# A hybrid decoder layer on one core: mixer output and memory keys computed with one load of the high weights for both halves of the input

## The chip, the cores and the metric

The kernel runs on one core of one Trainium2 chip, in one launch. The metric is device microseconds of an execution; the number for a kernel is the median of its runs. Before the change it is 1819.08 us, the median of 3 runs from 1818.16 to 1819.49.

## The reference, cut to what matters

A layer for 256 tokens of width 2048, all in float32: a token mixer, cross-attention into 256 memory tokens, and a gated channel mixer, each between two root-mean-square norms and added to the residual stream `x`.

```python
h = rms_norm(x, mix_pre_norm)
merged = ...                                  # mLSTM and RWKV-7 branches, gated
y = merged @ w_mix_out                        # 2048 x 2048: the mixer output
x = x + rms_norm(y, mix_post_norm)
h = rms_norm(x, xattn_pre_norm)
m = rms_norm(mem, mem_norm)
k, v = split(m @ xattn_wkv)                   # 2048 x 512 each: the memory's keys and values
q = h @ xattn_wq
o = softmax(q k / sqrt(128)) v                # 4 heads of 128
x = x + rms_norm(o @ xattn_wo, xattn_post_norm)
h = rms_norm(x, ffn_pre_norm)
x = x + rms_norm((gelu(conv(h @ w_up_gate)) * conv(h @ w_up_up)) @ w_down, ffn_post_norm)
```

## The kernel before

Every large product is made of three. A float32 weight and a float32 input are each split into a high part and a low part of the type fp32r, and the kernel adds high weight x high input, high weight x low input, and low weight x high input. `Feed` (L373) brings the weights in pieces of 128 x 1024 numbers, called sources here: a DMA into `raw` (three buffers), then ACT casts `raw` to `wh` (L402, the high part), then DVE subtracts `wh` from `raw` into `wl` (L423, the low part); `wh` and `wl` have four buffers each, in tiles of 1024 + 128 columns (`staged`, L391). All matmuls go through the helper `mm`, so they stand at L189 in the profile.

The program is a list of blocks, run one after the other by `run` (L435). A block of kind `fm` makes 512 output features for all 256 tokens, features on the partitions, into two PSUM banks of the pool `acc`, which has four; for each of the 16 slices `k` of the input and each of 4 groups of 128 features it issues three matmuls of 256 columns, each with its own weight load (below, a narrow triple). A block of kind `tm` puts tokens on the partitions and moves weights, 512 columns at a time. A block with `wide` makes 256 features: for each slice and group it issues one matmul of 512 columns, high weights against high and low input side by side, and one of 256 columns, low weights against high input (a wide pair). A bank then holds high and low products apart, and they have to be added when they leave PSUM. Before the change only 58 blocks of the channel mixer's first product are wide (`w_fw`); their `fw_evac` (L1627) lets ACT copy the low half to SBUF (tile `ul`) and DVE add the high half from PSUM (tile `us`).

The stages that the text speaks of stand in this order, with the tiles that name them in the profile: the mixer output `w_mo` (four `fm` blocks over `mgh` and `mgl`, evacuated by `y_evac`, L1268, which also adds up squares for the norm, `sty`); the memory's keys `w_xk` (one `fm` block over `mx`, evacuated by `kx_evac` into `kT`); the queries `w_xq` (one `fm` block over `qh` and `ql`); the memory's values `w_xv` (one `tm` block over `mx`, evacuated into `xv`); the attention output `w_xo` (four `fm` blocks over `oT`); then the channel mixer.

Everything beside the matmuls is written as Python generators, whose pieces `run` lets out between matmuls. A call of `side.half` (L107) is a half step: there are two for each source, in narrow and in wide blocks. At a half step one piece of the first waiting evacuation is issued, if a budget of estimated DVE and ACT time allows it, and then one piece of each chain that is due. Each engine executes its instructions in the order in which they were issued.

Between the keys and the queries stands `Residual` (L1294). It waits until the sum of squares of the mixer output is done: `column_of_sums` (L344) adds the two halves of `sty` on DVE (`fold`), waits `n` half steps (1 unless told otherwise), issues the small matmuls `st`, a DVE and a GpSimd instruction, and waits one half step more; then `Residual` issues the matmuls `stb`. From there it issues a piece every two half steps. Each of its pieces 0 to 7 lets DVE scale two slices of the mixer output (`z`), add them to the residual stream (`xr`), and split the sum into two slices of the queries' input, `qh` on ACT and `ql` on DVE. While it runs, the same DVE also makes the `wl` of every source. When it is near its end, squares of the new residual stream are summed (`stx`), and after the queries the softmax of the four heads runs as a chain of pieces under the values' matmuls: scores `xsc`, exponentials `spr`, transposes `xpT`, a copy `pT` on ACT. `need_o` (L1559) makes the attention output wait for the softmax, for `xv`, and for the matmuls `xo`, whose result is split into `oT`.

Of the kernel before, what the change touches and what calls it, by code (L numbers as in the profile page):

```python
# [9 lines left out]
F32 = mybir.dt.float32  # L10
F32R = mybir.dt.float32r
# [141 lines left out]
def _layer(ctx, tc, nc, d, dbg):  # L153
# [15 lines left out]
    def big(name, shape=None, dt=F32):  # L169
        return mp.tile(shape or [P, KD, S], dt, tag="big", bufs=2, name=name)  # L170
# [97 lines left out]
    def times(out, ps, row):  # L268
# [2 lines left out]
            row = bc(row, ps.shape[1])  # L271
        dve.tensor_mul(apart(out), halves(ps), apart(row))

    def bc(ap, n):
        return ap.unsqueeze(1).broadcast_to((ap.shape[0], n, ap.shape[1]))

# [96 lines left out]
    class Feed:  # L373
# [16 lines left out]

        def staged(self, name, r):  # L391

            w = wp.tile([P, 1024 + 128], F32R, tag=name, bufs=4, name=name)
            k, c = r.shape[1:]
            return w[:, 0:k * c].rearrange("p (k c) -> p k c", k=k)

# [843 lines left out]
    def br_evac(i, cb):  # L1240
        def gen(ps):
            sg = M["sg", i, cb]
            if cb == 0 and i == 0:
                M["pa"] = [U("pa0", [P, D]), U("pa1", [P, D])]
            if cb == 0 and i == 1:
                M["mg"] = [big("mgh", dt=F32R), big("mgl", dt=F32R)]
            for t in range(2):
                pa = M["pa"][t][:, cb * 512:cb * 512 + 512]
                if i == 0:
                    dve.tensor_mul(pa, ps[t], sg[t])  # L1250
                else:
                    dve.tensor_mul(sg[t], ps[t], sg[t])
                    dve.tensor_add(sg[t], sg[t], pa)
                yield
            if i == 0:
                return
            yield
            for t in range(2):
                q = aux("mT", [P, 4, P])
                for j in range(4):  # L1260
                    pe.transpose(q[:, j], sg[t][:, j * P:(j + 1) * P], ident)
                mg = [apart(M["mg"][j][:, cb * 4:cb * 4 + 4])[:, :, :, t * 64:t * 64 + 64] for j in range(2)]
                split(mg[0], mg[1], halves(q))
                yield
        return gen


    def y_evac(b, st, key, gname):  # L1268

        def gen(ps):  # L1270
            if b == 0:
                M[key] = [U("z0"), U("z1")]
            z = M[key][b // 2]
            late = b == 3 and key == "z2"
            if late:
                st.add(ps[0])
                st.last(ps[1], "bg0")
                st.column()
            for g in range(2):
                if not late:  # L1280
                    st.add(ps[g])
                for j in range(2):
                    m = (b % 2) * 4 + g * 2 + j
                    act.activation(z[:, m], ps[g][:, j], AF.Copy, scale=pcol(gname, b * 4 + g * 2 + j))
                if g or not late:
                    yield
            if b == 3 and not late:
                yield from st.column_of_sums()
        return gen

    def part(v, k2):
# [118 lines left out]
    sty = Stat("sty")  # L1410
    stm = Stat("stm", "ysb0")

    def mem_prep():
        mx = hT("mx")
        M["mh"], M["ml"] = mx[:, 0], mx[:, 1]
        ts = []
        for c in range(10):
            if c % 2 == 0 and c < 8:
                ts.append(C("mem", f"bg{c // 2 % 2}", [P, 4, S]))
                sp.dma_start(ts[c // 2], d["mem"][:, c * 2:c * 2 + 4])  # L1420
            if c >= 2:
                t = ts[c // 2 - 1][:, c % 2 * 2:c % 2 * 2 + 2]
                for j in range(2):
                    k = c * 2 - 4 + j
                    split_gain(M["mh"][:, k], M["ml"][:, k], t[:, j], pcol("mg", k))
                stm.add(t)
            yield
        yield from stm.finish()
# [20 lines left out]
    def load_x():  # L1449
        tables("natural_log_exp_and_others")  # L1450
        M["xr"] = [U("xr0"), U("xr1")]
        for i in range(2):
            sp.dma_start(M["xr"][i], d["x"][:, i * 8:i * 8 + 8])

    def mo_xs(k):
        if k == 12:
            side.need(br["task"])
        return M["mg"][0][:, k], M["mg"][1][:, k]

    for b in range(4):  # L1460
        block("fm", W("w_mo", b), mo_xs, y_evac(b, sty, "z1", "postg"),
              before=load_x if b == 1 else None)


    stx = Stat("stx")
# [4 lines left out]
        M["qh"] = big("qh", dt=F32R), big("ql", dt=F32R)  # L1470
        M["res"] = Residual(sty, "z1", stx, M["qh"][0], M["qh"][1], "xg", True)

    def kx_evac(ps):
        M["kT"] = [T2("kT") for _ in range(2)]
        for g in range(2):
            times(M["kT"][g], ps[g], stm.rb)
        yield

    def qx_evac(ps):
        yield from M["res"].wait(16)  # L1480
# [70 lines left out]
            xsplit(M["oT"][:, 0, h2 * 2:h2 * 2 + 2], M["oT"][:, 1, h2 * 2:h2 * 2 + 2], q)  # L1551
            yield

    block("fm", W("w_xk", 0), mxs, kx_evac, before=start_res1)
    block("fm", W("w_xq", 0), lambda k: M["res"].tile(k), qx_evac)
    xv = block("tm", W("w_xv", 0), mxs, vx_evac)
    st3 = Stat("st3")
# [69 lines left out]
    def fw_evac(f):  # L1627

        def gen(ps):
            cv = M["cv"]  # L1630
            us, lo = T2("us"), T2("ul")
            for i in range(2):
                act.copy(lo[:, i], ps[i][:, 1])
            for i in range(2):
                dve.tensor_add(us[:, i], ps[i][:, 0], lo[:, i])
# [36 lines left out]
    def asplit(k):  # L1672

        if k not in M["as"]:
            n = k // 2
            a = mp.tile([P, 1024 + 128], F32R, tag=f"au{n % 2}", bufs=1, name="as")[:, 112:112 + 1024]
            a = a.rearrange("p (i j s) -> p i j s", i=2, j=2)
            a, b_ = a[:, 0], a[:, 1]
            for j in range(2):
                split(a[:, j], b_[:, j], actile((k + j) % 64))  # L1680
                M["as"][k + j] = (a[:, j], b_[:, j])
        return M["as"][k]
# [128 lines left out]
def prepare(i):  # L1811
# [42 lines left out]
    o["w_mo"] = _blocks(f["w_mix_out"][0], 512)  # L1854
    kv = f["xattn_wkv"][0]
    o["w_xk"], o["w_xv"] = _blocks(kv[:, :512], 512), _blocks(_pairs(kv[:, 512:]), 512)
# [22 lines left out]
```

## Time and profile before

| | |
|---|---|
| median of 3 runs | 1819.08 us |
| the profiled execution | 1819.0 us |
| its span in the profile | 1817.2 us |
| TensorE matmul (PE) busy | 1802.2 us, 99% |
| TensorE weight load (PEld) busy | 1650.7 us, 91% |
| VectorE (DVE) busy | 1341.1 us, 74% |
| ScalarE (ACT) busy | 1069.8 us, 59% |
| GpSimd (POOL) busy | 30.6 us, 2% |
| granted TensorE clock, mean | 0.998 |

The span is what the profile shows; 1.8 us of the execution lie around it. Engines work beside one another, so busy shares do not add up. Ends of matmuls are modelled: a PE that is busy all the time can still leave room between its matmuls, and it is the distance from start to start that tells the rate.

### The profile page before, as it was taken

What the parts mean: (1) busy time and instruction counts of PE and PEld (TensorE: products, weight loads), DVE (VectorE), ACT (ScalarE), POOL (GpSimd) and SP (SyncE); (2) the same over time, 40 slices, a digit from 0 to 9 for tenths busy, and PEclk for the clock granted to TensorE, in tenths of its full rate; (3) what the DMA queues carried; (4) which work ended last, traced back from release to release, by engine and by line L of the source; (5) the groups of instructions that cost most, each with busy time, mean ns of one, the idle gap of its engine ahead of it and who ended that gap; (6) DMA issues with size and microseconds to landing.
All of it is one profiled execution on the core that took longest, in us unless ns stands there. A gap on an engine that the chain in (4) does not pass through costs nothing.

```text
span 1817.2 us, 30695 instructions
## 1 busy us (share of the span) xinstructions
PE 1802.2 (99%) x12062; PEld 1650.7 (91%) x12062; DVE 1341.1 (74%) x1938; ACT 1069.8 (59%) x1616; POOL 30.6 (2%) x53
## 2 busy tenths in 40 slices
PE   9999999999999999999999999999999999999998
PEld 9999988888888999899899999999999988888887
DVE  7879985665765757778888888878778776666665
ACT  6577455554644655666666667666556565555553
POOL 0100000100100000000000000000000000000000
PEclk9999999999999999999999999999999999999999
DMA  7655554354566765545566666666666666666664
GB/s 261 199 182 186 165 186 151 120 183 151 187 192 205 245 231 175 185 145 189 195 209 198 204 203 200 199 202 202 201 202 201 201 202 221 207 207 202 204 200 159
DMA packets 97889, 352.35 MB, mean 194 GB/s; under 512 B 11057, under 2 KB 11313, under 8 KB 97361
## 3 DMA queue, kind: packets, MB, share of 16 engines
q1 hardware_dynamic: 96496, 348.07, 60.4%
q8 instruction: 94, 1.54, 0.3%
q0 software_dynamic: 384, 1.18, 0.2%
q10 hardware_dynamic: 864, 1.15, 0.2%
q14 instruction: 51, 0.41, 0.1%
HBM read 347.73 MB, written 2.10 MB: 193 GB/s over the span
## 4 chain that ended last, share of the span: by engine, by line
PE 92%; DVE 4%; issue 1%; DMA 1%; ACT 1%; POOL 0%; DVEq 0%; POOLq 0%; ACTq 0%
PE fm L189 51%; PE tm L189 37%; DVE wl L423 1%; ACT wh L402 1%; DMA raw<-in_w_in_dram 0%; PE gram L189 0%; PE Y L189 0%; DVE ql L66 0%; DMA x<-in_x_dram 0%; PE lv L189 0%; DVE tg L66 0%; PE X L189 0%; PE zwa L189 0%; PE num L189 0%; PE gramA L189 0%
## 5 line engine op out<-in xcount | busy, mean ns | idle before, releaser
L423 DVE TENSOR_TENSOR wl<-raw,wh 128x1024 fp32r<-128x1024 f32 x640 | 781.4, 1222 | 315.8 <-ACT wh L402 311.8
L402 ACT CAST wh<-raw 128x1024 fp32r<-128x1024 f32 x640 | 670.2, 1049 | 390.5 <-PE fm L189 161.3
L189 PE MATMUL fm<-fx,wh 128*128 128x512 f32 (+1 forms) x2240 | 673.6, 364 | 0.0
L189 PE MATMUL fm<-fx,wl 128*128 128x256 f32 x2048 | 559.5, 273 | 1.3 <-DVE wl L423 1.1
L189 PEld LDWEIGHTS fm<-fx,wh 128*128 128x128 f32 x2240 | 409.5, 190 | 49.1 <-ACT wh L402 0.3
L189 PEld LDWEIGHTS fm<-fx,wl 128*128 128x128 f32 x2048 | 393.6, 192 | 2.8 <-DVE wl L423 2.8
L189 PE MATMUL tm<-wh,as 128*128 128x512 f32 x1024 | 304.6, 379 | 0.0
L189 PE MATMUL tm<-wh,hx 128*128 128x512 f32 x768 | 232.0, 384 | 0.0
L189 PEld LDWEIGHTS tm<-wh,as 128*128 128x128 f32 x1024 | 193.5, 189 | 27.4
L189 PE MATMUL tm<-wl,as 128*128 128x512 f32 x512 | 194.0, 379 | 0.0
L189 PE MATMUL fm<-hx,wh 128*128 128x256 f32 x1120 | 192.2, 278 | 0.8 <-ACT wh L413 0.8
L189 PEld LDWEIGHTS fm<-hx,wh 128*128 128x128 f32 x1120 | 171.4, 193 | 2.2 <-ACT hx L66 1.1
L189 PEld LDWEIGHTS tm<-wh,hx 128*128 128x128 f32 x768 | 141.9, 189 | 19.5
L189 PE MATMUL fm<-hx,wl 128*128 128x256 f32 x560 | 154.9, 277 | 0.0
L189 PE MATMUL tm<-wl,hx 128*128 128x512 f32 x384 | 145.5, 379 | 0.0
L189 PEld LDWEIGHTS tm<-wl,as 128*128 128x128 f32 x512 | 96.8, 189 | 13.7
L189 PEld LDWEIGHTS fm<-hx,wl 128*128 128x128 f32 x560 | 108.2, 193 | 0.2 <-DVE wl L414 0.2
L66 ACT CAST as<-ac 128x256 fp32r<-128x256 f32 x128 | 45.5, 402 | 106.1 <-PE tm L189 106.1
L66 DVE TENSOR_TENSOR as<-ac,as 128x256 fp32r<-128x256 f32 x128 | 48.6, 422 | 54.9 <-ACT as L66 54.9
L66 ACT COPY ul<-fm 128x256 f32<-128x256 f32 x116 | 40.5, 374 | 73.2 <-PE fm L189 73.2
L189 PEld LDWEIGHTS tm<-wl,hx 128*128 128x128 f32 x384 | 72.6, 189 | 10.3
L189 PE MATMUL fm<-mgh,wh 128*128 128x256 f32 x256 | 70.7, 276 | 0.0
(356 smaller groups left out, 1958.0 us busy)
## 6 DMA issues: line engine op xcount, KB each, us to landing
raw<-in_w_fw_dram SPq DMA_DIRECT2D x232, 512.0 KB, 4.1
raw<-in_w_in_dram SPq DMA_DIRECT2D x160, 512.0 KB, 4.0
raw<-in_w_fd_dram SPq DMA_DIRECT2D x128, 512.0 KB, 3.8
raw<-in_w_br_dram SPq DMA_DIRECT2D x32, 512.0 KB, 3.9
raw<-in_w_mo_dram SPq DMA_DIRECT2D x32, 512.0 KB, 3.5
raw<-in_w_fu_dram SPq DMA_DIRECT2D x24, 512.0 KB, 3.8
raw<-in_w_xk_dram SPq DMA_DIRECT2D x8, 512.0 KB, 3.3
raw<-in_w_xq_dram SPq DMA_DIRECT2D x8, 512.0 KB, 3.5
```

Of the source, the lines that this page charges most:

```text
L66: return f(out, *a, **k)
L189: pe.matmul(out, lhsT, rhs, start=start, stop=stop, skip_group_check=True)
L402: nc.scalar.copy(wh, r)
L423: nc.vector.tensor_sub(wl, r, self.st[self.nl][0])
```

## The change

The first quarter of the mixer output stays one narrow block. The other three quarters become six wide blocks of 256 features, with their weights in a new array `w_mw`. The memory's keys become two wide blocks. A new helper `whole` does what `fw_evac` did to put the halves of a bank together, in one tile `lo` with two buffers, and the channel mixer uses it too. `y_evac` takes squares and gains from that tile in the wide blocks, and `kx_evac` scales from it. For wide matmuls high and low input have to lie in one tile, so `mgh` and `mgl` become two tiles that are cut by slice instead, each with high and low. The sum of squares behind the mixer output waits 4 half steps instead of 1. The tiles of `wh`, `wl` and `as` lose their 128 spare columns, and with the pools' sizes all buffers behind them move.

```diff
+    def whole(ps):
+
+        w = mp.tile([P, 2, S], F32, tag="lo", bufs=2, name="lo")
+        for i in range(2):
+            act.copy(w[:, i], ps[i][:, 1])
+        for i in range(2):
+            dve.tensor_add(w[:, i], ps[i][:, 0], w[:, i])
+        return w
...
-            w = wp.tile([P, 1024 + 128], F32R, tag=name, bufs=4, name=name)
+            w = wp.tile([P, 1024], F32R, tag=name, bufs=4, name=name)
...
-                M["mg"] = [big("mgh", dt=F32R), big("mgl", dt=F32R)]
+                M["mg"] = [big(f"mg{j}", [P, 2, 8, S], F32R) for j in range(2)]
...
-    def y_evac(b, st, key, gname):
+    def y_evac(b, st, key, gname, wide=False):
...
+            if wide:
+                ps = [whole(ps)]
...
-            for g in range(2):
+            for g, v in enumerate(ps):
                 if not late:
-                    st.add(ps[g])
+                    st.add(v)
                 for j in range(2):
-                    m = (b % 2) * 4 + g * 2 + j
-                    act.activation(z[:, m], ps[g][:, j], AF.Copy, scale=pcol(gname, b * 4 + g * 2 + j))
-                if g or not late:
+                    m = b * len(ps) * 2 + g * 2 + j
+                    act.activation(z[m // 8][:, m % 8], v[:, j], AF.Copy, scale=pcol(gname, m))
+                if g == len(ps) - 1 or not late:
                     yield
-            if b == 3 and not late:
-                yield from st.column_of_sums()
+            if b == (7 if wide else 3) and not late:
+                yield from st.column_of_sums(4)
...
-    for b in range(4):
-        block("fm", W("w_mo", b), mo_xs, y_evac(b, sty, "z1", "postg"),
-              before=load_x if b == 1 else None)
+    block("fm", W("w_mo", 0), mo_xs, y_evac(0, sty, "z1", "postg"))
+    for b in range(2, 8):
+        block("fm", W("w_mw", b - 2), mo_xs, y_evac(b, sty, "z1", "postg", True), before=load_x if b == 2 else None,
+              cols=256, wide=mgp)
...
-    def kx_evac(ps):
-        M["kT"] = [T2("kT") for _ in range(2)]
-        for g in range(2):
-            times(M["kT"][g], ps[g], stm.rb)
-        yield
+    def kx_evac(g):
+        def gen(ps):
+            if g == 0:
+                M["kT"] = [T2("kT") for _ in range(2)]
+            times(M["kT"][g], whole(ps), stm.rb)
+            yield
+        return gen
...
-    block("fm", W("w_xk", 0), mxs, kx_evac, before=start_res1)
+    for g in range(2):
+        block("fm", W("w_xk", g), mxs, kx_evac(g), before=None if g else start_res1, cols=256,
+              wide=lambda k: mx[:, :, k])
...
-            a = mp.tile([P, 1024 + 128], F32R, tag=f"au{n % 2}", bufs=1, name="as")[:, 112:112 + 1024]
+            a = mp.tile([P, 1024], F32R, tag=f"au{n % 2}", bufs=1, name="as")
```

The change moves instructions in three places. The first is on DVE, from the fold of the sum of squares to the first piece of `Residual`; `z_6873` and `xr_6867` are the first of the two tiles of the scaled mixer output and of the residual stream. Before:

```order
L66 TENSOR_TENSOR sty<-sty 128x256
L423 TENSOR_TENSOR wl<-raw,wh 128x1024
L66 TENSOR_SCALAR var<-st 128x2
L423 TENSOR_TENSOR wl<-raw,wh 128x1024
L66 TENSOR_TENSOR z_6873<-z_6873,stb 128x256
L66 TENSOR_TENSOR xr_6867<-xr_6867,z_6873 128x256
L66 TENSOR_TENSOR z_6873<-z_6873,stb 128x256
L66 TENSOR_TENSOR xr_6867<-xr_6867,z_6873 128x256
L66 SCALAR_TENSOR_TENSOR ql<-xr_6867,par,qh 128x256 x2
```

On DVE at the same place now; `lo<-fm,lo` adds the halves of the first keys' block:

```order
L66 TENSOR_TENSOR sty<-sty 128x256
L432 TENSOR_TENSOR wl<-raw,wh 128x1024 x2
L66 TENSOR_SCALAR var<-st 128x2
L432 TENSOR_TENSOR wl<-raw,wh 128x1024
L66 TENSOR_TENSOR lo<-fm,lo 128x256 x2
L66 TENSOR_TENSOR kT<-lo,stm_b 128x512
L66 TENSOR_TENSOR z_6873<-z_6873,stb 128x256
L66 TENSOR_TENSOR xr_6867<-xr_6867,z_6873 128x256
L66 TENSOR_TENSOR z_6873<-z_6873,stb 128x256
L66 TENSOR_TENSOR xr_6867<-xr_6867,z_6873 128x256
L66 SCALAR_TENSOR_TENSOR ql<-xr_6867,par,qh 128x256 x2
```

One more `wl` and the whole evacuation of the first keys' block now stand ahead of the first `z`.

The second place is on PE, at the end of the values' block (`tm`), where the last head's transposes `xpT` and then the matmuls `xo` stand; a minus is before, a plus is now:

```order
 L189 MATMUL tm<-wl,mx 128x512
-L1535 MATMUL xpT<-con,spr 128x128 x4
-L189 MATMUL tm<-wh,mx 128x512 x2
-L189 MATMUL tm<-wl,mx 128x512
-L189 MATMUL tm<-wh,mx 128x512 x2
-L189 MATMUL tm<-wl,mx 128x512
-L189 MATMUL tm<-wh,mx 128x512 x2
-L189 MATMUL tm<-wl,mx 128x512
-L189 MATMUL tm<-wh,mx 128x512 x2
-L189 MATMUL tm<-wl,mx 128x512
+L1555 MATMUL xpT<-con,spr 128x128 x4
 L189 MATMUL xo<-pT,xv 128x256 x8
```

The last 12 matmuls of the values stood between `xpT` and `xo`; now they stand ahead of both. The scores' chain is later by as many matmuls from `st<-stx` on, throughout the values' block.

The third place is on ACT, at the same point of the program; `pT` copies transposes, `xv` evacuates the values, `oT` splits the result of `xo`. Before:

```order
L66 COPY pT<-xpT 128x512
L402 CAST wh<-raw 128x1024
L66 COPY pT<-xpT 128x512
L66 ACTIVATE xv<-tm,stm_c 128x512 x2
L66 CAST oT<-xo 128x512 x2
```

On ACT at the same place now:

```order
L66 ACTIVATE spr,psum<-xsc,mx 128x256 x2
L411 CAST wh<-raw 128x1024
L66 COPY pT<-xpT 128x512 x2
L66 ACTIVATE xv<-tm,stm_c 128x512 x2
L66 CAST oT<-xo 128x512 x2
```

The copies of the last two heads now follow one another, and the two instructions of `xv` still stand behind the last copy.

More of the change, by code (lines that the diff above doesn't have):

```diff
@@ L1261, in gen @@
                     pe.transpose(q[:, j], sg[t][:, j * P:(j + 1) * P], ident)
-                mg = [apart(M["mg"][j][:, cb * 4:cb * 4 + 4])[:, :, :, t * 64:t * 64 + 64] for j in range(2)]
+                k4 = slice(cb % 2 * 4, cb % 2 * 4 + 4)
+                mg = [apart(M["mg"][cb // 2][:, j, k4])[:, :, :, t * 64:t * 64 + 64] for j in range(2)]
                 split(mg[0], mg[1], halves(q))
@@ L1272, in gen @@
                 M[key] = [U("z0"), U("z1")]
-            z = M[key][b // 2]
+            z = M[key]
+            if wide:
+                ps = [whole(ps)]
             late = b == 3 and key == "z2"
@@ L1411, in _layer @@
     stm = Stat("stm", "ysb0")
+    mx = None
     def mem_prep():
+        nonlocal mx
         mx = hT("mx")
@@ L1453, in load_x @@
             sp.dma_start(M["xr"][i], d["x"][:, i * 8:i * 8 + 8])
+    mgp = lambda k: M["mg"][k // 8][:, :, k % 8]
     def mo_xs(k):
@@ L1457, in mo_xs @@
             side.need(br["task"])
-        return M["mg"][0][:, k], M["mg"][1][:, k]
-    for b in range(4):
-        block("fm", W("w_mo", b), mo_xs, y_evac(b, sty, "z1", "postg"),
-              before=load_x if b == 1 else None)
+        return mgp(k)[:, 0], mgp(k)[:, 1]
+    block("fm", W("w_mo", 0), mo_xs, y_evac(0, sty, "z1", "postg"))
+    for b in range(2, 8):
+        block("fm", W("w_mw", b - 2), mo_xs, y_evac(b, sty, "z1", "postg", True), before=load_x if b == 2 else None,
+              cols=256, wide=mgp)
     stx = Stat("stx")
@@ L1630, in gen @@
             cv = M["cv"]
[L1631 to L1635, printed above, removed]
+            us = whole(ps)
             dve.tensor_mul(us, us, bc(stf.rb, 2))
@@ L1853, in prepare @@
     o["w_br"] = np.concatenate([_blocks(_pairs(f[n][0]), 512) for n in ("w_branch_a", "w_branch_b")], 0)
-    o["w_mo"] = _blocks(f["w_mix_out"][0], 512)
+    o["w_mo"], o["w_mw"] = _blocks(f["w_mix_out"][0][:, :512], 512), _blocks(f["w_mix_out"][0][:, 512:], 256)
     kv = f["xattn_wkv"][0]
-    o["w_xk"], o["w_xv"] = _blocks(kv[:, :512], 512), _blocks(_pairs(kv[:, 512:]), 512)
+    o["w_xk"], o["w_xv"] = _blocks(kv[:, :512], 256), _blocks(_pairs(kv[:, 512:]), 512)
     o["w_xq"] = _blocks(f["xattn_wq"][0], 512)
```

## The prediction

> **What bounds the kernel now.** I read the page first: busy times, then the chain that ended last.
>
> ```profile
> PE 1802.2 (99%) x12062; PEld 1650.7 (91%) x12062; DVE 1341.1 (74%) x1938; ACT 1069.8 (59%) x1616; POOL 30.6 (2%) x53
> PE 92%; DVE 4%; issue 1%; DMA 1%; ACT 1%; POOL 0%; DVEq 0%; POOLq 0%; ACTq 0%
> ```
>
> TensorE bounds the kernel, by the rate at which it starts matmuls. Shares over the span hide what matters here, so the second view is busy time by stage: a stretch of the mixer output, the keys up to the sum of squares (697 to 705 us), the rest of the keys (to 719.8), the queries in two parts (to 742.2), the values (to 769.4), `xo`, and the start of the channel mixer.
>
> ```profile
> core 0: us, PE busy (x) PEld busy (x) DVE busy (x) ACT busy (x) POOL busy (x), PEclk, DMA share, GB/s
> 654.00:676.00 22.00, 22.00 (x200) 22.00 (x199) 11.58 (x12) 10.82 (x16) 0.00 (x0) 1.00 0.61 196
> 697.00:705.00 8.00, 7.92 (x71) 7.71 (x69) 4.90 (x7) 4.98 (x9) 0.69 (x1) 1.00 0.62 193
> 705.00:719.80 14.80, 14.80 (x135) 14.80 (x134) 14.39 (x25) 9.39 (x15) 0.00 (x0) 1.00 0.45 141
> 719.80:732.00 12.20, 11.79 (x103) 11.41 (x103) 12.10 (x20) 7.73 (x13) 0.00 (x0) 1.00 0.42 136
> 742.20:769.40 27.20, 26.68 (x131) 22.79 (x129) 19.49 (x32) 16.91 (x33) 0.00 (x0) 1.00 0.60 193
> 794.60:801.50 6.90, 6.20 (x37) 5.69 (x36) 2.74 (x9) 3.11 (x7) 0.70 (x1) 0.75 0.24 78
> ```
>
> From 705 to 732 us DVE is busy 26.5 of 27.0 us: in this stage it is as full as PE. The timeline of PE in the queries' block shows that it is already the one that is waited for.
>
> ```profile
> 727.89 0.28 PE L189 MATMUL fm<-ql,wh 128*128 128x256 f32 x1
> 728.24 0.38 PE L189 MATMUL fm<-qh,wl 128*128 128x256 f32 x1
> ...
> 730.91 0.28 PE L189 MATMUL fm<-ql,wh 128*128 128x256 f32 x1
> 731.52 0.38 PE L189 MATMUL fm<-qh,wl 128*128 128x256 f32 x1 [0.33 <-DVE wl L423]
> ```
>
> From one row to the next it should take 0.11 us (the next rows give that); it takes 0.35 and 0.61, so PE loses 0.24 + 0.50 = 0.74 us, both times at a first use of `wl`.
>
> **The change part by part.** *The rate.* Timeline of PE in the mixer output, 24 matmuls apart, and of ACT in the channel mixer, where the copies `ul` come once in each wide block:
>
> ```profile
> 651.74 0.28 PE L189 MATMUL fm<-mgl,wh 128*128 128x256 f32 x1
> 654.42 0.28 PE L189 MATMUL fm<-mgl,wh 128*128 128x256 f32 x1
> ```
> ```profile
> 1099.46 0.70 ACT L66 COPY ul<-fm 128x256 f32<-128x256 f32 x2 [1.34 <-PE fm L189]
> 1109.94 0.70 ACT L66 COPY ul<-fm 128x256 f32<-128x256 f32 x2 [1.34 <-PE fm L189]
> ```
>
> 2.68 / 24 = 0.1117 us a matmul, so a narrow triple takes 0.335 us. A wide block has 16 slices x 2 groups = 32 pairs and takes 10.48 us: 0.3275 a pair. The change removes 256 weight loads and matmuls (192 in the mixer output, 64 in the keys) and gains 7.5 ns for each: 192 x 7.5 ns = 1.44 us and 64 x 7.5 ns = 0.48 us. Bounds: nothing, if the new tiles stream worse, and the same 1.9 us, since these are whole blocks with nothing left to hide. The Trainium skill, "TensorE: Matmul & The Clock Gate", section "Back-to-back issue gap", gives a start-to-start distance of the columns over 2.4 GHz plus 2.5 ns; by that a triple is 327.5 ns and a pair 325, the gain 0.64 us, and the sum below 1823.0. The trace does not agree on the triple (335 ns), so the rows stand.
>
> *The evacuations* of the six wide blocks add to each two copies on ACT and two additions on DVE. A block has 10.48 us and four sources beside it, and in the mixer output DVE is busy 11.58 and ACT 10.82 of 22 us; the bank is wanted again two blocks later. I cost this at nothing there. Without that cover it would be the copies and additions themselves, about 1.5 us a block.
>
> *The sum of squares and the Residual.* This is where a wait changes. The next views are the groups on the tiles `mx` and `qh` (first and last start), DVE's timeline from the first `z` on, and the channel mixer's additions.
>
> ```profile
> L189 PE MATMUL fm<-mx,wh x128: 275/275/356, 697.0 to 719.5; 128*128 128x256 f32 x128
> L189 PE MATMUL fm<-qh,wh x64: 275/275/275, 719.7 to 741.8; 128*128 128x256 f32 x64
> ```
> ```profile
> 705.39 0.41 DVE L66 TENSOR_TENSOR z<-z,stb 128x256 f32<-128x256 f32 x1
> ...
> 708.73 1.22 DVE L423 TENSOR_TENSOR wl<-raw,wh 128x1024 fp32r<-128x1024 f32 x1
> ...
> 712.65 1.20 DVE L423 TENSOR_TENSOR wl<-raw,wh 128x1024 fp32r<-128x1024 f32 x1
> ...
> 715.92 1.23 DVE L423 TENSOR_TENSOR wl<-raw,wh 128x1024 fp32r<-128x1024 f32 x1
> ...
> 719.23 1.21 DVE L423 TENSOR_TENSOR wl<-raw,wh 128x1024 fp32r<-128x1024 f32 x1
> ...
> 722.51 1.22 DVE L423 TENSOR_TENSOR wl<-raw,wh 128x1024 fp32r<-128x1024 f32 x1
> 723.64 1.28 DVE L66 TENSOR_TENSOR kT<-fm,stm_b 128x512 f32<-128x512 f32 x2
> ...
> 726.97 1.22 DVE L423 TENSOR_TENSOR wl<-raw,wh 128x1024 fp32r<-128x1024 f32 x1
> ...
> 730.25 1.21 DVE L423 TENSOR_TENSOR wl<-raw,wh 128x1024 fp32r<-128x1024 f32 x1
> ...
> 732.78 1.22 DVE L423 TENSOR_TENSOR wl<-raw,wh 128x1024 fp32r<-128x1024 f32 x1
> ```
> ```profile
> 1099.87 0.76 DVE L66 TENSOR_TENSOR us<-fm,ul 128x256 f32<-128x256 f32 x2 [0.49 <-ACT ul L66]
> 1100.65 0.69 DVE L66 TENSOR_TENSOR us<-us,stf_b 128x512 f32<-128x512 f32 x1
> ```
>
> I count from the first matmul of the keys, 697.0. Before, `z` starts at 8.4 and the queries at 22.7; the keys' 192 matmuls are 21.4 of that, so the small matmuls `st` and `stb` with their waits take 1.3. Of these I keep 1.1, since after 4 half steps the fold should not be waited for. Now the queries start at 64 x 0.3275 + 1.1 = 22.1, which is 0.6 us sooner. But `z` stands on DVE behind the evacuation of the first keys' block, and that block ends at 32 x 0.3275 + 1.1 = 11.6. By the channel mixer's rows it is 1.19 us from the first copy to the end of the additions, then 0.6 for one `kT`: `z` starts at 13.4, 5.0 us later than before.
>
> From there DVE works without a gap, before and now, one piece of `Residual` and one `wl` in turn. Before, the `wl` starts lie 3.3, 7.3, 10.5, 13.8, 17.1, 21.6, 24.9 and 27.4 us behind `z`. They are now one source further, since one more `wl` was made ahead: the second is for the queries' first source, the eighth for their seventh. The evacuation of the second keys' block, 1.4 us with two additions and one `kT`, comes ahead of the fifth `wl` instead of 1.2 behind it: 18.5, 21.8, 25.1, 27.6. With 1.25 us for the `wl` itself the second to the eighth are ready at 21.9, 25.2, 28.5, 33.1, 36.4, 39.7 and 42.2. PE wants the first at 22.3 (the third matmul of a source) and each further one 24 x 0.1117 = 2.68 later, plus what it has already waited. It waits 0 for the first, then 0.2, 0.6, 1.9, 0.7, 0.6, and 0 for the seventh: 4.0 us in place of 0.74. With the 0.6 gained ahead the stage costs +2.7 us net. Bounds: -0.6 - 0.7 = -1.3, if DVE found the time after all, and +3.7, if the copies on ACT are late by 1 us. I take +2.7, since every duration in it is a row of this stage.
>
> *The end of the values.* Timelines of PE and ACT:
>
> ```profile
> 766.24 0.60 PE L1535 MATMUL xpT<-con,spr 128*128 128x128 f32 x4
> 766.59 0.68 PE L189 MATMUL tm<-wh,mx 128*128 128x512 f32 x2
> ...
> 769.05 0.38 PE L189 MATMUL tm<-wl,mx 128*128 128x512 f32 x1
> 769.62 0.48 PE L189 MATMUL xo<-pT,xv 128*128 128x256 f32 x1 [0.19 <-ACT xv L66]
> ```
> ```profile
> 767.17 0.58 ACT L66 COPY pT<-xpT 128x512 f32<-128x512 f32 x1
> 768.88 1.28 ACT L66 ACTIVATE xv<-tm,stm_c 128x512 f32<-128x512 f32 x2 [1.13 <-PE tm L189]
> ```
>
> Before, 12 matmuls cover the copy `pT`, and `xo` starts 0.35 us behind the last one's slot (769.05 + 0.22). Now the transposes stand behind these matmuls (0.35 us of PE that is only moved), the copy starts when they end, 0.6 us after their start (their row), and takes 0.58; `xv` follows on the same engine, and `xo` starts 0.74 behind the start of `xv` (769.62 - 768.88). That is about 1.9 us from the first transpose to `xo`, where it was 0.35 + 0.35; and the second `xo` waits for the second half of `xv` another 0.3. I take +1.4, between +0.6 (only copy and transposes show) and +2.0.
>
> What is left (the same instructions in the channel mixer, DMAs of the same size and count, buffers that moved) I take as zero.
>
> **The sum** is made against the profiled execution, 1819.0 us (span 1817.2 and 1.8 around it), 0.1 below the median: -1.4 (mixer output) + 2.7 (keys and queries) + 1.4 (values) = +2.7: **1821.7 us**. The bound for no change, about what a measurement of this kernel can tell, is 0.2%, 3.6 us: 1815.4 to 1822.7.
>
> **The rivals.** *DVE does not reach PE.* The late `z` is caught up and only `xo` costs: 1819.0 - 1.4 - 1.3 + 1.4 = 1817.7. For it speaks that PE lost only 0.74 us in this stage; against it that DVE is full in the rows from 705 on.
> *Neither wait shows:* 1819.0 - 1.4 - 1.3 = 1816.3, or 1814.6 if the slow clock of 0.75 over 6.9 us at the channel mixer's start, 1.7 us at most, falls away too.
> *Slower, by the clock.* A row of the stages shows a stretch of the channel mixer with idle time of PE:
>
> ```profile
> 860.00:900.00 40.00, 38.69 (x246) 34.65 (x245) 35.05 (x58) 24.04 (x38) 0.00 (x0) 1.00 0.52 172
> ```
>
> The waits of PE in the queries, near 2 us in one place, cost a window of slow clock, as the stage from 794.6 shows one, with 0.75 of the clock: 1.7 us more, 1823.4, and 1824.5 with the bounds above. It decides if PE's idle time of about 2 us in one piece is enough; the 1.3 us of this row left the clock at 1.00. The Trainium skill ("TensorE: Matmul & The Clock Gate", "Why this matters for your kernels") asks for no idle gap above some 3 us; by that this rival does not happen; this row agrees, but no run here shows a gap of 2 us.
> *The pairs do not gain* in the new tiles `mg0` and `mg1`: 1821.7 + 1.4 = 1823.1.
> *The addresses.* With the spare columns gone, all `wh` and `wl` lie at other distances. If PE streamed 1% slower by it, the time would be 1837; against it, matmuls over four `wh` buffers in turn keep one distance of 0.1117.
>
> **How the numbers follow.** Forecast 0.5, DVE does not reach PE 0.17, neither wait 0.12, clock 0.12, no gain 0.06, addresses 0.03. The likeliest is 1821.7. The range runs from 1816.6, which leaves out most of the third case, to 1824.5, which takes in the clock. Faster: half of "neither wait", 0.06. Slower: the clock 0.12, the addresses 0.03, "no gain" 0.06, and 0.11 from the forecast's upper bounds: 0.32. The same: 0.62.
>
> **What would show it.** In the profile after: `mg0` and `mg1` against `wh` with 512 columns, and copies `lo` 10.5 us apart; the first `z` near 13 us behind the first keys' matmul; DVE busy to over 95% until the queries end; PE waiting for `wl` about 4 us in the queries, most at their fourth source; near 1.9 us from the last `xpT` to `xo`. The prediction is wrong if PE waits less than 2 us in the queries, if distances of matmuls in the channel mixer differ from before, or if another stage moves by over 1 us.

## The result, and the profile after

The kernel after takes 1822.38 us (median of 16 runs, 1820.84 to 1824.76) against 1819.09 us for the kernel before (16 runs, 1818.16 to 1820.97); the ratio is 1.0018, 95% interval 1.0011 to 1.0025. The runs of after lie in two groups, 7 from 1820.8 to 1821.5 and 9 from 1822.3 to 1824.8. The profiled one is the shortest of the first group: 1820.84 us, span 1819.0.

The busy times and the chain that ended last, after:

```profile
PE 1799.9 (99%) x11806; PEld 1641.1 (90%) x11806; DVE 1347.0 (74%) x1954; ACT 1075.6 (59%) x1632; POOL 31.5 (2%) x53
PE 92%; DVE 4%; ACT 2%; issue 1%; DMA 0%; POOL 0%; SPq 0%; DVEq 0%; POOLq 0%; ACTq 0%
```

The 256 matmuls are gone, and shares over the span say nothing more. The mixer output first: ACT's timeline, where the copies `lo` come once in each wide block.

```profile
674.13 0.70 ACT L66 COPY lo<-fm 128x256 f32<-128x256 f32 x2 [0.82 <-PE fm L189]
684.61 0.70 ACT L66 COPY lo<-fm 128x256 f32<-128x256 f32 x2 [1.31 <-PE fm L189]
```

A block takes 10.48 us, 0.3275 a pair, as in the channel mixer. From the first matmul of the mixer output to the first of the keys it is 87.52 us before and 86.08 after: 1.44 us less.

Next the groups on `mx` and `qh` (first and last start), which with the 64 matmuls of each group date the blocks, and DVE's timeline between them.

```profile
L189 PE MATMUL fm<-mx,wh x64: 382/382/462, 695.2 to 717.1; 128*128 128x512 f32 x64
L189 PE MATMUL fm<-qh,wh x64: 275/275/275, 717.4 to 742.8; 128*128 128x256 f32 x64
```
```profile
702.81 0.15 DVE L66 TENSOR_SCALAR var<-st 128x2 f32<-128x2 f32 x1
704.73 1.22 DVE L432 TENSOR_TENSOR wl<-raw,wh 128x1024 fp32r<-128x1024 f32 x1 [1.77 <-ACT wh L411]
707.24 0.76 DVE L66 TENSOR_TENSOR lo<-fm,lo 128x256 f32<-128x256 f32 x2 [1.28 <-ACT lo L66]
708.03 0.79 DVE L66 TENSOR_TENSOR kT<-lo,stm_b 128x512 f32<-128x512 f32 x1
708.74 0.41 DVE L66 TENSOR_TENSOR z<-z,stb 128x256 f32<-128x256 f32 x1
...
712.15 1.22 DVE L432 TENSOR_TENSOR wl<-raw,wh 128x1024 fp32r<-128x1024 f32 x1
```

The sum of squares is ready at 702.81, but `z` starts at 708.74, 13.5 us behind the first keys' matmul (8.4 before): it stands behind the evacuation of the first keys' block. Ahead of that, DVE idles 1.77 + 1.28 us. The next `wl` (712.15) stands behind the first piece of `Residual`, which will matter below. What PE then waits for, from the keys to `xo` (us in total, times, longest; idle time counts from the modelled end of the matmul ahead, so it is shorter than what the starts lose), and its timeline at the queries' fourth source:

```profile
PE fm L189 <- DVE wl L432: 2.9, 5, 1.8
PE xo L189 <- ACT xv L66: 1.3, 1, 1.3
PE xsc L189 <- DVE qT L66: 0.6, 1, 0.6
```
```profile
726.60 0.28 PE L189 MATMUL fm<-ql,wh 128*128 128x256 f32 x1
728.64 0.38 PE L189 MATMUL fm<-qh,wl 128*128 128x256 f32 x1 [1.76 <-DVE wl L432]
```

Before, the first of these waits was 0.3, the last 0.5, and `xo` waited 0.2. The end of the values, on PE and on ACT:

```profile
769.89 0.60 PE L1555 MATMUL xpT<-con,spr 128*128 128x128 f32 x4
771.76 1.06 PE L189 MATMUL xo<-pT,xv 128*128 128x256 f32 x3 [1.27 <-ACT xv L66]
```
```profile
770.53 0.59 ACT L66 COPY pT<-xpT 128x512 f32<-128x512 f32 x1 [2.15 <-PE xpT L1555]
771.01 1.27 ACT L66 ACTIVATE xv<-tm,stm_c 128x512 f32<-128x512 f32 x2
```

No matmul stands between the last transposes and `xo` any more; it starts 1.87 us behind them.

In the table, stages run from the first matmul of one to the first of the next, in the profiled execution of each kernel; the values end at `xo`, and where the matmuls `st<-stx` stand directly ahead of the values they count as their start. "Sum" is the four together against before. Medians are of 11 runs, of 16 for the first two rows; measured beside the experiments, the kernel before stood at 1818.91 to 1819.03.

| kernel | mixer output | keys | queries | values | sum | median us | ratio, 95% interval |
|---|---|---|---|---|---|---|---|
| before | 87.52 | 22.77 | 22.38 | 27.50 | | 1819.09 | |
| after | 86.08 | 22.23 | 25.67 | 28.65 | +2.46 | 1822.38 | 1.0018, 1.0011 to 1.0025 |
| e1_wait3 | 86.08 | 22.01 | 25.73 | 28.05 | +1.70 | 1820.85 | 1.0013, 1.0005 to 1.0022 |
| e2_keys_narrow | 86.08 | 22.64 | 22.23 | 30.50 | +1.28 | 1822.24 | 1.0014, 1.0005 to 1.0023 |
| e3_before_wait4 | 87.52 | 22.33 | 23.55 | 28.13 | +1.36 | 1820.06 | 1.0008, 0.9998 to 1.0017 |
| e4_after_again | 86.10 | 22.23 | 25.77 | 28.73 | +2.66 | 1821.53 | 1.0018, 1.0009 to 1.0027 |
| e5_fill | 86.08 | 22.23 | 26.07 | 29.49 | +3.70 | 1821.68 | 1.0017, 1.0008 to 1.0026 |
| e6_mixer_alone | 86.08 | 23.69 | 22.45 | 27.50 | -0.45 | 1819.78 | 1.0007, 0.9998 to 1.0016 |
| e7_wait6 | 86.08 | 22.28 | 23.31 | 28.89 | +0.39 | 1819.47 | 1.0000, 0.9992 to 1.0009 |
| e8_wait2 | 86.08 | 23.33 | 24.60 | 27.70 | +1.54 | 1820.66 | 1.0011, 1.0003 to 1.0020 |
| e9_wait3_cover | 86.08 | 22.35 | 24.56 | 26.82 | -0.36 | 1819.81 | 1.0002, 0.9993 to 1.0011 |
| e10_middle_blocks | 86.56 | 22.77 | 22.34 | 27.81 | -0.69 | 1819.08 | 0.9999, 0.9990 to 1.0008 |
| e11_no_spare | 87.52 | 22.77 | 22.34 | 27.43 | -0.11 | 1819.09 | 0.9997, 0.9988 to 1.0006 |
| e12_z_behind_wl | 86.08 | 21.85 | 24.88 | 28.20 | +0.84 | 1819.75 | 1.0007, 0.9998 to 1.0016 |

### The profile page after: what moved, and what is told of

It reads as the page before. It is cut to its first block, busy times and chain, and to the rows that moved or that the text cites. A ratio compares the mean times of both kernels' runs of the same rounds, so it can differ in the third digit from the quotient of the medians.

```text
span 1819.0 us, 30218 instructions
## 1 busy us (share of the span) xinstructions
PE 1799.9 (99%) x11806; PEld 1641.1 (90%) x11806; DVE 1347.0 (74%) x1954; ACT 1075.6 (59%) x1632; POOL 31.5 (2%) x53
## 3 DMA queue, kind: packets, MB, share of 16 engines
q10 hardware_dynamic: 864, 1.15, 0.2%
## 4 chain that ended last, share of the span: by engine, by line
PE 92%; DVE 4%; ACT 2%; issue 1%; DMA 0%; POOL 0%; SPq 0%; DVEq 0%; POOLq 0%; ACTq 0%
PE fm L189 51%; PE tm L189 37%; DVE wl L432 1%; ACT wh L411 1%; PE gram L189 0%; PE Y L189 0%; DVE z L66 0%; DMA wsm<-in_w_sm_dram 0%; PE lv L189 0%; DVE ql L66 0%; DVE tg L66 0%; PE X L189 0%; PE zwa L189 0%; DVE xr L66 0%; PE num L189 0%
## 5 line engine op out<-in xcount | busy, mean ns | idle before, releaser
L66 ACT COPY lo<-fm 128x256 f32<-128x256 f32 x132 | 46.0, 374 | 78.6 <-PE fm L189 78.6
L189 PE MATMUL fm<-mg,wh 128*128 128x512 f32 (+1 forms) x320 | 84.9, 340 | 0.0
```

What stands on the lines that cost most here:

```text
L66: return f(out, *a, **k)
L189: pe.matmul(out, lhsT, rhs, start=start, stop=stop, skip_group_check=True)
```

## The experiments

**A shorter wait.** The kernel after, one half step sooner.

```diff
-                yield from st.column_of_sums(4)
+                yield from st.column_of_sums(3)
```

> The sum of squares waits 3 half steps instead of 4; all else as after the change. In the order on DVE the first z then stands ahead of the evacuation of the first keys' block. Theory 'DVE is late': the gapless work on DVE starts about 1.4 us sooner (10.7 instead of 12.0 us behind the first matmul of the keys), so PE waits for wl in the queries about 2.3 us instead of 3.7, and xo waits as after the change: a profiled time near 1819.4 us. Rival 'the waits in the queries come from something that does not hang on when z starts' (DMA, ACT's casts): queries as long as after the change, 25.7 us, and 1820.8 us.

`z` came 2.25 us sooner (11.27), and the queries took as long as in after. DVE's timeline, where the first row is the first `z`:

```profile
707.02 0.41 DVE L66 TENSOR_TENSOR z<-z,stb 128x256 f32<-128x256 f32 x1
...
710.39 0.76 DVE L66 TENSOR_TENSOR lo<-fm,lo 128x256 f32<-128x256 f32 x2
711.19 0.79 DVE L66 TENSOR_TENSOR kT<-lo,stm_b 128x512 f32<-128x512 f32 x1
711.90 1.21 DVE L432 TENSOR_TENSOR wl<-raw,wh 128x1024 fp32r<-128x1024 f32 x1
```

The evacuation now stands behind the first piece, and still ahead of the `wl`. That `wl` ends 17.36 us behind the first keys' matmul, in after 18.16: of the 2.25 us only 0.8 reach it. They are lost again at the queries' seventh source, where two additions `stx` stand ahead of the `wl` and in after one. The start of `z` by itself does not set PE's wait, so the first theory failed. The rival's numbers came (25.7 and 1820.8 us), but not the causes it named: from `z` to the end of the queries no `wl` waits for ACT or for a DMA.

**The keys narrow again,** with the mixer output wide and a wait of 4.

```diff
-            times(M["kT"][g], whole(ps), stm.rb)
+            times(M["kT"][g], ps[g], stm.rb)
...
-    for g in range(2):
-        block("fm", W("w_xk", g), mxs, kx_evac(g), before=None if g else start_res1, cols=256,
-              wide=lambda k: mx[:, :, k])
+    block("fm", W("w_xk", 0), mxs, kx_evac, before=start_res1)
```

> The keys stay one narrow block, the mixer output is wide as after the change, the wait is 4 half steps. Theory 'DVE is late': z starts 11.6 us behind the first matmul of the keys with no evacuation ahead of it, PE waits 1.5 us in the queries (0.74 before the change, 3.7 after), keys and queries together take 45.7 us (45.1 before, 47.9 after); xo has no matmuls of the values ahead of it and still costs 1.1 us; the mixer output is 1.44 us shorter than before: about 1819.2 us. Rival 'the wide mixer output itself brings the loss' (its evacuations): still near 1821 us.

The queries are back at 22.23: PE loses 0.6 us there by waits for `wl`, where 1.5 was expected. But the values take 3.0 us more than before: 1.9 at the first scores `xsc`, 1.0 at `xo`. PE's row of `xsc`, then DVE's:

```profile
750.98 1.13 PE L189 MATMUL xsc<-kT,qT 128*128 128x256 f32 x4 [2.44 <-DVE qT L66]
```
```profile
749.10 1.23 DVE L432 TENSOR_TENSOR wl<-raw,wh 128x1024 fp32r<-128x1024 f32 x1 [3.67 <-ACT wh L411]
750.24 1.28 DVE L66 TENSOR_TENSOR qT<-fm,stx_b 128x512 f32<-128x512 f32 x2
```

`qT` stands behind a `wl` that waits 3.67 us for its `wh`, which ACT could not cast before its DMA had landed. DVE is not full here; an instruction that is ready stands behind one that is not. Neither theory had this wait. The median, 1822.24, is above both times expected, with 6 of 11 runs from 1822.2 on; the profiled execution took 1820.22.

**The wait alone,** in the kernel before: `column_of_sums(4)`, nothing else.

> The kernel before with one change, the wait of the sum of squares of 4 half steps in place of 1; no wide block in mixer output or keys. Theory 'the wait moves Residual and the scores': z starts 13.9 us behind the first matmul of the keys instead of 8.4, PE waits 2.0 us in the queries, xo follows the transposes of two heads without any matmul of the values between and costs 1.8 us: 1821.8 us. Rival 'the wait is hidden, only the wide keys' evacuation costs': 1819.0 us.

Its waits of PE:

```profile
PE xo L189 <- ACT xv L66: 1.3, 1, 1.3
PE fm L189 <- DVE wl L423: 1.1, 3, 0.4
```

`z` starts at 13.92, later than in after, and yet the queries lose only 1.2 us. `xo` loses its cover as in after. So the wait alone makes the end of the values dearer, and adds to the queries about a third of what after adds. The rest does not come from the wide keys as such. Here the `wl` of the keys' last source stands ahead of the first `z` (it ends 14.00 us behind the first keys' matmul), in after behind the first piece (18.16); e7_wait6, with wide keys and that `wl` ahead of `z`, adds 0.9 us to the queries. The measured 1820.06 lies between the two expectations.

**The same kernel again,** unchanged, to see what a second set of runs gives.

> The changed kernel once more, for its single times: 16 of them had 7 between 1820.8 and 1821.5 us and 9 between 1822.3 and 1824.8. Theory 'clock': the long ones hold one or two stretches of 3.4 us at half clock that the short ones lack, behind the 1.9 us wait of PE in the queries or the 1.5 us wait of xo; a profile of a long one shows them there. Rival 'the waits themselves vary' (DMA): the long ones have longer waits and the same clock.

1821.53, with 7 of 11 runs from 1821.2 to 1821.7 and 4 from 1823.0 to 1824.7. The stages repeat within 0.1 us, and so do the waits. The two groups repeat too. The profiled execution belongs to the shorter group, so it can't show what the longer ones hold.

**Is it the clock behind the long wait?** `keep_warm(16)` ahead of the matmul that waits.

```diff
+                            if b is bq and ci == 3 and kj == 0 and m == 0:
+                                keep_warm(16)
```

> The kernel after, with 16 small matmuls on a spare bank (0.11 us each, 1.75 us in all, by the warm rows of the channel mixer's start) put ahead of the matmul that waits 2.0 us for wl in the queries. They add instructions and no waiting, so the profiled time stays at that of after, 1820.8 to 1821.5. If a long wait of TensorE brings a stretch of slow clock in some executions (these would be after's executions of 1822.3 to 1824.8), all executions now lie between 1820.5 and 1822.0. If the long executions have another cause, about half of them stay above 1822.

```profile
726.40 3.74 PE L189 MATMUL warm<-ones 128*128 128x128 f32 x32
```

The profile has two matmuls for each of the 16 asked for, so the filler is twice as long as the expectation counted: 3.5 us lost at this place, where the wait had cost 1.9. PE no longer waits there, and 4 of 11 runs still lie from 1822.9 to 1824.9. So the long wait in the queries is not what parts the runs. The stages became 1.2 us longer than after's: the queries 0.4, since the later sources now wait less, and the values 0.8, since PE waits at `xsc` (1.4 us in place of 0.6).

**The mixer output alone.** As e2_keys_narrow, with a wait of 2 half steps, which are shorter in time behind a block of half the size.

```diff
-                yield from st.column_of_sums(4)
+                yield from st.column_of_sums(2)
```

> Mixer output wide, keys narrow as before, and the sum of squares 2 half steps behind, which with the narrower last block is the place it had before. Theory (DVE's work and place behind the keys, and the lost cover of xo, cost what the mixer output gained): z 8.4 us behind the first keys' matmul, PE waits in the queries under 1 us, xo starts 0.6 behind its neighbour as before, span 1817.2 - 1.4 = 1815.8, time 1817.6, all executions in one group. Rival (the removed spare columns or the new tiles cost something elsewhere): 1819 or more.

Queries and values are those of before, `xo` has its cover again, but the keys took 0.9 us more:

```profile
PE st L189 <- DVE sty L66: 0.9, 1, 0.9
PE xsc L189 <- DVE qT L66: 0.5, 1, 0.5
PE fm L189 <- DVE wl L432: 0.5, 2, 0.3
```

The last wide block is put together, squared and folded before `st` can start, and that takes longer than 2 half steps. A longer wait is needed there; 4 was more than needed. The stages gain 0.45 us, but the median, 1819.78, is not below before's.

**A longer wait:** `column_of_sums(6)` in the kernel after.

> The kernel after with a wait of 6 half steps in place of 4. z moves by two half steps (2.6 us) to some 16.5 us behind the first keys' matmul; with DVE full from z on, PE waits 6.3 us in the queries in place of 3.7 and the first wait grows: 1821.3 + 2.6 + up to 0.5 for the later end of the values = 1824 if nothing else happens. If a long wait of TensorE brings a stretch of slow clock, its profile shows a row of half clock right behind the longest wait, and most executions are 1.5 to 3 us longer still, 1825.5 to 1827. If DVE catches up somewhere, 1822.

All expectations failed: it became 2 us faster than after. PE's wait for `wl` fell from 2.9 to 1.0 us, though `z` starts at 13.84, 0.3 later than in after. DVE's timeline and the waits:

```profile
707.56 0.79 DVE L66 TENSOR_TENSOR kT<-lo,stm_b 128x512 f32<-128x512 f32 x1
708.27 1.22 DVE L432 TENSOR_TENSOR wl<-raw,wh 128x1024 fp32r<-128x1024 f32 x1
709.40 0.41 DVE L66 TENSOR_TENSOR z<-z,stb 128x256 f32<-128x256 f32 x1
```
```profile
PE xo L189 <- ACT xv L66: 1.3, 1, 1.3
PE fm L189 <- DVE wl L432: 1.0, 3, 0.4
```

A `wl` now stands between `kT` and `z`. In after the same one stands behind the first piece: counted from the first keys' matmul it ends at 18.16 there, at 13.92 here. Since `wl` and pieces take turns from there on, each later `wl` has one piece less ahead of it, and up to the queries' sixth source each is 2.9 to 3.6 us sooner. PE waits for the `wl`, not for the pieces. This was read after the run, so e12_z_behind_wl tests it.

**A wait of 2 with wide keys:** `column_of_sums(2)` in the kernel after.

> The kernel after with a wait of 2 half steps in place of 4: the keys stay wide, z stands ahead of the evacuation of the first keys' block, and st of the next sum comes back to its place ahead of the values, so that matmuls cover the last copy pT again. Theory: z 9.5 us behind the first keys' matmul, but the evacuation still comes ahead of the second wl, so that wl is ready some 2 us sooner than in after: PE waits 2 us in the queries in place of 3.7, xo costs nothing more: 1821.3 - 1.7 - 1.2 = 1818.4. If the place of z alone set the queries' wait, 1817.2 (waits of 0.7); if the additions of the wide keys alone set it, 1820.1 (waits of 3.7).

`z` at 9.29 and the cover of `xo` (values 27.70, near before's) came as the theory said. The `wl` did not come 2 us sooner: the queries' first is ready 22.74 us behind the first keys' matmul, in after 22.11. PE loses 2.85 us by waits for `wl`, between the 2 of the theory and the 3.7 of the additions alone. The fold was not ready, as in e6_mixer_alone: the wait at `st` made the keys 1.1 longer than after's. The profiled execution is one of the long ones, 1825.0 us, and shows where such a one loses its time: its mixer output starts at 614.2 us in place of 609.1, and from there on it runs like the others. PE's timeline:

```profile
31.76 0.92 PE L189 MATMUL st<-ones,st 128*128 128x1 f32 x4 [2.62 <-DVE st L66]
32.54 0.77 PE L189 MATMUL fm<-hx,wh 128*128 128x256 f32 x2
33.10 0.42 PE L189 MATMUL fm<-hx,wl 128*128 128x256 f32 x1
33.32 0.63 PE L189 MATMUL fm<-hx,wh 128*128 128x256 f32 x2
```

And the busy times of that stretch, with the granted clock (PEclk):

```profile
30.00:40.00 10.00, 8.24 (x45) 8.24 (x45) 5.20 (x7) 2.88 (x3) 0.70 (x1) 0.66 0.88 258
```

In the program's first block PE waits 2.62 us (0.2 in after's profile), and behind that three matmuls take about 0.64 us in place of 0.335, for 6.8 us. In the same profile a wait in the queries, 2.0 us from start to start, is followed by full clock.

**A wait of 3, and the cover kept.** As e6_mixer_alone with 3 half steps, and `stx` one half step sooner.

```diff
-                yield from st.column_of_sums(2)
+                yield from st.column_of_sums(3)
...
-                yield from self.st2.rows(6, 1)
+                yield from self.st2.rows(5, 1)
```

> Mixer output wide, keys narrow, a wait of 3 half steps, and the next sum of squares (stx) one half step sooner, so that its matmuls stand ahead of the values as before and 12 matmuls cover the last copy pT. Theory (the fold must be over when st comes, DVE must have its wl done ahead of z, and xo needs its cover): st does not wait (1.1 us in e6_mixer_alone), z 9.8 us behind the first keys' matmul with one more wl ahead of it, PE waits under 1 us in the queries, up to 0.3 at stx, xo as before: span 1816.0, time 1817.8, faster than before and after. Rival (DVE is too late for stx, or something outside this stage costs as in e6_mixer_alone): 1819 or more.

```profile
PE fm L189 <- DVE wl L432: 1.1, 3, 0.4
PE st L189 <- DVE stx L66: 0.7, 1, 0.7
PE xo L189 <- ACT xv L66: 0.2, 1, 0.2
```

`st` of the mixer output no longer waits and `xo` is covered, but the queries lose 2.2 us by waits for `wl` and, at their end, for `stx`, out of 2.5 us won in the other three stages. The median is 1819.81. The rival's time came, and its first reason brought less than half of the queries' loss: 0.9 us at `stx`, 1.3 by the waits for `wl`.

**The two middle quarters of the mixer output wide,** the last quarter and the keys as before.

```diff
-            if b == (7 if wide else 3) and not late:
-                yield from st.column_of_sums(4)
+            if b == 3 and not wide and not late:
+                yield from st.column_of_sums()
...
-    for b in range(2, 8):
+    for b in range(2, 6):
         block("fm", W("w_mw", b - 2), mo_xs, y_evac(b, sty, "z1", "postg", True), before=load_x if b == 2 else None,
               cols=256, wide=mgp)
+    block("fm", W("w_mo", 1), mo_xs, y_evac(3, sty, "z1", "postg"))
```

> Only the two middle quarters of the mixer output are wide; the last quarter, the keys and the waits are as before, so the order on DVE and PE behind the last mixer output block is the one of before. Theory: 128 pairs x 7.5 ns = 0.96 us less in the mixer output and nothing else: span 1816.2, time 1818.1. Rival (the wide blocks cost elsewhere, by their tiles or the missing spare columns): 1819 or more.

The mixer output is 0.96 us shorter, as 128 pairs should be, keys and queries are unchanged, and `xsc` waits 0.3 longer. The profiled execution, 1817.70 us, is the shortest of all kernels here; the median, 1819.08 against 1819.03, shows no gain. No version beat the kernel before beyond the interval.

**The spare columns alone.**

```diff
-            w = wp.tile([P, 1024 + 128], F32R, tag=name, bufs=4, name=name)
+            w = wp.tile([P, 1024], F32R, tag=name, bufs=4, name=name)
...
-            a = mp.tile([P, 1024 + 128], F32R, tag=f"au{n % 2}", bufs=1, name="as")[:, 112:112 + 1024]
+            a = mp.tile([P, 1024], F32R, tag=f"au{n % 2}", bufs=1, name="as")
```

> The kernel before without the 128 spare columns of wh, wl and as, and nothing else. Theory: the addresses cost nothing, 1819.0, matmuls 0.1117 us apart everywhere. Rival by the addresses: the stages or the distances of matmuls differ, or more executions lie over 1820.5 than the 11 of 82 of the kernel before.

1819.09, no run above 1819.8, and all four stages within 0.1 us: in the kernel before, the addresses cost nothing.

**`z` behind the `wl`.** The kernel after with `st` where it was, and only `z` one half step later.

```diff
-                yield from st.column_of_sums(4)
+                yield from st.column_of_sums(4, 2)
```

> The kernel after, with st at its place (4 half steps behind) and only z, the first piece of Residual, one half step later. On DVE one more wl then stands between the evacuation of the first keys' block and z, as in e7_wait6. Theory (what counts is the wl that stands ahead of z, since DVE would idle there otherwise): z at 13.8 us behind the first keys' matmul, 0.3 later than in after, and yet the queries' first wl is ready 3 us sooner; PE waits 1.5 us in the queries in place of 3.7, 1821.3 - 2.2 + up to 0.4 in the values = 1819.3. Rival (the later st, or the 8 transposes together at the end, made e7_wait6 faster): waits of 3.7 or more, 1821.5.

```profile
707.60 0.84 DVE L66 TENSOR_TENSOR kT<-lo,stm_b 128x512 f32<-128x512 f32 x1
708.31 1.27 DVE L432 TENSOR_TENSOR wl<-raw,wh 128x1024 fp32r<-128x1024 f32 x1
709.44 0.47 DVE L66 TENSOR_TENSOR z<-z,stb 128x256 f32<-128x256 f32 x1
```
```profile
PE fm L189 <- DVE wl L432: 2.1, 5, 0.7
PE xo L189 <- ACT xv L66: 1.3, 1, 1.3
```

`z` starts later (14.28 behind the first keys' matmul), and the stages take 1.6 us less than after's. The queries' first `wl` is ready 3.1 us sooner. The total came near what was expected, 1819.75, and the rival, 1821.5, falls; the parts did not come as expected: the queries became 0.8 us shorter, not 2.2, the keys 0.4 and the values 0.45. PE still loses 2.9 us by waits for `wl` (3.7 in after), now at the queries' fourth to eighth source, where it was the second to sixth: the pieces that were passed still have to be done before the stage ends. Idle time of DVE that is filled, which the expectation named, is the smaller part: `z` starts 0.75 us later for a `wl` of 1.2. The rest of the gain comes from the order.

## Why the prediction was right

1821.7 was forecast, and 1822.4 measured, inside the range and, with 0.18%, within the bound for no change, though with an interval that leaves 1.0000 out. By its own steps:

- **The rate.** -1.44 forecast, 86.08 - 87.52 = -1.44 measured, with 0.3275 us a pair. The gain of 0.64 in all that the prediction worked out by the Trainium skill ("TensorE: Matmul & The Clock Gate", "Back-to-back issue gap") did not come. That section gives this distance for a matmul by itself and says that with a weight load for each matmul it counts too little when columns are few; the prediction left this out. The triple agrees with it (335 ns, not 327.5); the pair stays near the distance (327.5 against 325).
- **The keys.** -0.6 forecast, -0.54 measured; `z` at 13.4 forecast, 13.5 measured. That PE would not wait at `st` holds, and e6_mixer_alone shows what the longer wait buys: 0.9 us.
- **The queries.** Waits of 0, 0.2, 0.6, 1.9, 0.7, 0.6, 0 forecast for the first to the seventh source; the distances of matmuls give 0, 0.3, 0.5, 1.9, 0.5, 0.5, 0: 3.7 us in place of 4.0. The stage grew by 3.29, where 4.0 - 0.74 = 3.26 was forecast; that the two are so near is luck. The matmul behind each wait starts 0.1 us late too, five times in after and twice before, which the working left out, and this makes up for the 0.3 by which the waits were too long.
- **Why the queries wait** was told too simply. The prediction blamed that `z` comes 5.0 us later. e1_wait3, with `z` 2.25 sooner, waits as long as after; e7_wait6 and e12_z_behind_wl, with `z` later, wait less. What counts is how many pieces of `Residual` stand ahead of each `wl` on DVE: in after one more than in those two. The working went by the order of after, so its number was near. DVE is as full as it says: 98% busy from `z` to the end of the queries.
- **The values.** +1.4 forecast, +1.15 measured: 1.87 us from transposes to `xo` (1.9 forecast), and the second `xo` did not wait another 0.3. e6_mixer_alone, with `stx` back ahead of the values, has before's 27.50.
- **The rest**, forecast as zero, was -0.6 us in the profiled execution: 0.3 ahead of the mixer output and 0.3 from `xo` on. The latter is 0.8 less in the stretch where before has its half clock (794.6 to 801.5) and after has full clock, and 0.5 more behind it.
- **The rivals.** "DVE does not reach PE" and "neither wait" fall with 2.9 us of waits for `wl`. "The pairs do not gain" and "the addresses" fall with 86.08 us and e11_no_spare. "By the clock" named a time within after's longer group, 1823.4, and the wrong place: waits of 2.0 us from start to start in the queries of after, e1_wait3, e4_after_again and e8_wait2 are followed by full clock, and with that wait filled the long runs stay. The long execution that was profiled, one of e8_wait2, lost its 5 us in the program's first block; none of after's was profiled.

So +2.46 us in the four stages is shown, by profiles and twice by runs: e4_after_again's median is 2.6 above before's. The profiled execution of after is only 1.8 longer than before's, by the -0.6 of the rest; that the 16 runs give 3.3 comes from the longer group. The sum had neither, and that the total came so near, 0.7 from the median, is in part luck. Why the longer group is larger there (9 of 16, then 4 of 11) than for the kernel before (17 of 124 runs over 1820.3) is open: the first block has the same instructions in both, and the spare columns alone don't bring it (none of 11 runs of e11_no_spare).

## What to carry to other kernels

Merging matmuls pays what the rate says (here 7.5 ns for each weight load saved), but the separate halves must be put together again, and that work lands on the engine that may be the one waited for at the next stage. Where an engine takes turns between work that the bound engine waits for and work that is wanted later, look at which comes first when a late piece sets in: one turn too late puts a whole piece ahead of every later turn. A wait counted in steps should be tried in both directions, since in the four stages here 3 half steps cost 0.8 us less than 4, and 6 cost 2.1 less.

## What the runs showed of the hardware

A slow clock can follow a shorter wait than I had thought. Behind 2.62 us of waiting in the first block of e8_wait2, two stretches of 3.4 us ran at half clock; in e9_wait3_cover one stood behind 1.47 us at the same place:

```profile
30.26 0.61 PE L189 MATMUL st<-ones,st 128*128 128x1 f32 x4 [1.47 <-DVE st L66]
```
```profile
31.90:35.30 3.40, 3.40 (x18) 3.40 (x17) 1.23 (x1) 1.22 (x2) 0.37 (x1) 0.50 1.04 274
```

In the kernel before, a stretch at half clock at the start of the channel mixer has no wait over 0.55 us of PE in the 4 us ahead of it:

```profile
798.10:801.50 3.40, 3.40 (x18) 3.28 (x16) 2.44 (x7) 1.05 (x2) 0.00 (x0) 0.50 0.00 0
```

Yet idle times of 1.28 us in the first block of e6_mixer_alone, of 1.76 in the queries of after and of 2.44 at `xsc` in e2_keys_narrow left it at 1.00. The length of one wait alone does not decide it; what does is not shown. The Trainium skill ("TensorE: Matmul & The Clock Gate", "Why this matters for your kernels") asks for no idle gap over some 3 us between bursts of matmuls; these slow stretches stood behind shorter ones.
